# Softmax denominators of a FoX head pair: fp32 products over 128 rows, or folded to 64 rows and summed as two fp32r parts

## The chip, the cores and the metric

The kernel runs on one core of a Trainium2 chip. The metric is the device time of one execution in microseconds (us). Every line of the profile that computes is "L176", since a helper records the operations first and emits them later; tiles are therefore told apart by their names.

## The reference, cut to what matters

A two-layer decoder trunk over a sequence of 2048 tokens with model width 1024: layer 0 mixes tokens by gated linear attention (GLA), layer 1 by forgetting attention (FoX) with 16 heads of width 64. After each mixer a gated per-layer embedding (PLE) is added. The part that the change touches is the softmax of FoX:

```
logits = q . k / sqrt(d) + c[t] - c[s]          (c = cumsum(log f), causal)
probs  = softmax(logits)
o      = probs @ v
out    = (o * silu(g)) @ w_out
```

The kernel computes exp(logit - bound) without normalizing and divides the output by the sum of these exponentials over all keys: one sum for each query and head.

## The kernel before, in words

Tokens are taken in NCH = 4 chunks of T = 512 queries. Everything is held feature-major: 128 partitions by 512 tokens. fp32 precision is kept with fp32r products: an operand is split into a high part (a cast on ScalarE) and a low part (the rest, a subtraction on VectorE or GpSimd), and two or three products replace one.

**Order of the work.** The kernel is a set of generators ("streams") that `Streams.run` interleaves: `dense` (projections, output projection, PLE), `maxima` (an upper bound of each head's logits), `attention`, and short ones that are spawned with the highest priority. A stream yields what it waits for: a mark such as ("den", c, u), a free PSUM bank, or tiles that are done. The planner gives each operation a modelled start on its engine, and `flush` emits all operations in order of these starts. So every engine's order is fixed at build time, by this plan; on the chip the engines only wait for one another by semaphores. A change of one operation moves the order of all engines from there on.

**Attention.** `attention` goes through the 16 heads of a chunk. For each block of 128 keys it computes S transposed (keys on partitions, queries along the row) in a PSUM bank, exponentiates it on ScalarE into `Ph` and again in full precision, and adds the full-precision exponentials up, 128 keys by 512 queries. Two blocks in three are added by VectorE into `acc`; every third goes to GpSimd, which adds into `ag`. After the last block GpSimd adds `ag` to `acc`. So `acc` holds 128 partial sums for each query, and the sum over its 128 rows is the denominator. The products with V run two blocks later (LAG = 2) and `join` then takes the finished head.

**Denominators** (`join`, lines 1414 to 1457). Heads 2u and 2u+1 share one output tile `op`: rows 0 to 63 and 64 to 127. When the second head of a pair is done, a stream `rest` is spawned. It multiplies the two `acc` tiles in fp32 with `onesh`, two 128x128 matrices of which the first has ones in columns 0 to 63, the second in columns 64 to 127, and accumulates both into one bank `den`. Row r of this bank is then the sum of the head to which row r of `op` belongs. The bank is inverted (Ln, Exp, one Newton step), multiplied with `op` and the gate `sg`, and the result goes to the output projection, as the parts `ogh` and `ogl` or through DRAM (`os`).

**Where things wait.** `attention` waits at every odd head for the denominators of the pair before. `rest` waits for the pair's gate, ("sg1", c, u), before it takes a bank. There are three buffers of `acc` and one of `op`. `total` (line 375) is the helper that sums over partitions with two fp32r products; the q/k norms use it with `onesb` (ones in the two diagonal 64x64 blocks). Its parts `kh` and `kl` have two buffers each, which the q and k parts also use. `ple_last` keeps seven projections in buffers that attention no longer needs.

Of the kernel before, what the change touches and what calls it, by code (L numbers as in the profile page):

```python
# [11 lines left out]
F32 = mybir.dt.float32  # L12
# [8 lines left out]
P = 128  # L21
# [50 lines left out]
class Streams:  # L72
# [134 lines left out]
    def at(self, *aps):  # L207

        return self.over([self.hist[k][0] for x in aps for k in self.parts(x) if k in self.hist and self.hist[k][0]])
# [102 lines left out]
def trunk_kernel(ctx: ExitStack, tc: tile.TileContext, a: dict, out: bass.AP, layers: int = 2):  # L312
# [46 lines left out]
    def psa(name):  # L359
        return banks[sq_.take()]  # L360
# [431 lines left out]
    def ple_last(p, c):  # L792


        f, keep = L["f"], []
        for m in range(KT):
            if m % 2 == 0:
                w = wnext("wp")
            pj = yield from proj(p, w, m)
            tag = ("P0", "ag", "acc", "acc")[m // 2] if m < KT - 1 else "hx"  # L800
            keep.append((f if m < KT - 1 else acts).tile([P, T], F32, tag=tag, name="pk", bufs={"P0": 2, "ag": 2, "acc": 3, "hx": HX}[tag]))
            nc.scalar.copy(keep[m], pj)
            give(pj)
        yield ("hn1", c)

        def tail(m, pg, cs):
            e = sigmoid(pg, "ny", 2)
            give(pg)
            nc.vector.tensor_tensor(e, e, keep[m][:, cs], ALU.mult)
            nc.vector.tensor_tensor(hr[:, m, cs], hr[:, m, cs], e, ALU.add)  # L810

        s, first = SumSq(), []
        for i in range(2):
            for m in range(N_G):
                if i == 0:
                    yield bank()
                    first.append(psa("pg"))
                yield from half(first[m], og, "wg", i)
        for m in range(KT - 1):
            pg = first[m] if m < N_G else (yield from unit("pg", og, "wg"))  # L820
            tail(m, pg, slice(0, T))
            s.add(hr[:, m], nc.vector)
            if m < POOL_F:

                nc.scalar.mul(hr[:, m], hr[:, m], gcol[:, G_FIN, m : m + 1])

        w = [wnext("wg") for _ in range(2)]
        m, hw = KT - 1, T // 2
        halves = [slice(i * hw, (i + 1) * hw) for i in range(2)]
        pgs = []  # L830
        for cs in halves:
            yield bank()
            pg = psa("pg")[:, 0:hw]
            yield from steps([(w[k // 4][a][:, k % 4], og[b][:, k, cs]) for k in range(KT) for a, b in ((0, 0), (0, 1), (1, 0))], pg, 0, 24)
            tail(m, pg, cs)
            q = t2("nsq", "sq", 2)[:, 0:hw]
            nc.scalar.activation(q, hr[:, m, cs], AF.Square)
            pgs.append(q)
        for cs, q in zip(halves, pgs):
            yield bank()  # L840
            pn = psa("nq_p")[:, 0:hw]
            yield at(s.acc)
            mm(pn, ones, s.acc[:, cs], stop=False)
            yield at(q)
            mm(pn, ones, q, start=False)
            r = rsqrt(pn, 1.0 / D)
            give(pn)
            for k0 in range(0, KT, 2):
                for k in (k0, k0 + 1):
                    if k < POOL_F:  # L850
                        nc.gpsimd.tensor_tensor(hr[:, k, cs], hr[:, k, cs], r, ALU.mult)
                    else:
                        nc.vector.scalar_tensor_tensor(hr[:, k, cs], hr[:, k, cs], gcol[:, G_FIN, k : k + 1], r, ALU.mult, ALU.mult)
                nc.sync.dma_start(out[c][:, k0 : k0 + 2, cs], hr[:, k0 : k0 + 2, cs])
# [277 lines left out]
    def setup1():  # L1132
        sq_.flush()
        gx.close()
        f, fc = sbuf("f", 2), sbuf("fc", 1)
        L["f"] = f
        free.extend([fc.tile([P, 4, P], F32R, name=f"wx{x}{i}") for x in "hl"] for i in range(WX))

        L["onesb"] = fc.tile([P, P], F32R, name="onesb")
        onesb = L["onesb"].bitcast(F32)  # L1140
        nc.vector.memset(onesb, 0.0)
        nc.vector.memset(onesb[0:64, 0:64], 1.0)
        nc.vector.memset(onesb[64:128, 64:128], 1.0)
        L["onesh"] = onesh = fc.tile([P, 2, P], F32, name="onesh")
        nc.vector.memset(onesh, 0.0)
        nc.vector.memset(onesh[:, 0, 0:64], 1.0)
        nc.vector.memset(onesh[:, 1, 64:128], 1.0)

        L["lim"] = lim = fc.tile([P, T + P], BF16, name="lim")
        nc.vector.memset(lim, 0.0)  # L1150
        nc.vector.memset(lim[:, T:], -BIG)
        nc.gpsimd.affine_select(lim[:, T - P : T], lim[:, T - P : T], pattern=[[-1, P]], compare_op=ALU.is_ge, fill=-BIG, base=0, channel_multiplier=1)
        L["limT"] = limT = fc.tile([P, 2 * P], BF16, name="limT")
        nc.vector.memset(limT, 0.0)
        nc.gpsimd.affine_select(limT, limT, pattern=[[1, 2 * P]], compare_op=ALU.is_ge, fill=-BIG, base=-P, channel_multiplier=-1)
        L["qkg"] = qkg = fc.tile([P, 2], F32, name="qkg")
        nc.sync.dma_start(qkg, a["qkgain"])
        nc.vector.tensor_scalar(qkg[:, 0:1], qkg[:, 0:1], -(HD ** -0.5), None, ALU.mult)
        nc.vector.tensor_scalar(qkg[:, 1:2], qkg[:, 1:2], -1.0, None, ALU.mult)
        L["bf"] = bf = fc.tile([FH, 1], F32, name="bf")  # L1160
        nc.sync.dma_start(bf, a["fox_bf"])
        wfr = t2("wfr", "sq", 2)[:, 0 : KT * FH].rearrange("p (k n) -> p k n", n=FH)
        nc.sync.dma_start(wfr, a["fox_wf"])
        L["wf"] = wf = fc.tile([P, KT, 48], F32R, name="wf")
        nc.vector.memset(wf.bitcast(F32), 0.0)
        split(wf[:, :, 0:16], wf[:, :, 32:48], wfr, nc.vector)

        L["As"] = [fc.tile([P, T], F32R, name=f"As{i}") for i in range(NQ)]  # L1170
        L["Es"] = [fc.tile([P, T], F32R, name=f"Es{i}") for i in range(NQ)]
        L["Dm"] = [fc.tile([P, T], F32R, name=f"Dm{i}") for i in range(2)]
        L["Dc"] = [fc.tile([P, T], F32R, name=f"Dc{i}") for i in range(2)]
        for t in (*L["Es"], *L["Dm"], *L["Dc"]):
            nc.vector.memset(t[64:128].bitcast(F32), 0.0)
        for t in L["Dc"]:
            rdma(t[66:67].rearrange("o (t n) -> o t n", n=P), ones[0:4])
        for t in L["Es"]:
            nc.vector.memset(t[64:66].bitcast(F32), 1.0)
        L["carry"] = fc.tile([FH, 1], F32, name="carry")  # L1180
        nc.vector.memset(L["carry"], 0.0)

        L["KS"] = [dram.tile([FH, 130, T], F32R, name=f"KS{c}") for c in range(NCH)]

        L["QS"] = [[dram.tile([P, T], F32R, name=f"QS{h}_{c}") for c in range(NCH)] for h in range(FH)]
        L["VS"] = [[dram.tile([8, P, 4, P], F32R, name=f"VS{i}_{c}") for c in range(NCH)] for i in range(2)]
# [144 lines left out]
    def attention():  # L1331
        nxt = None
        for i in range(NCH * FH):
# [1 line left out]
            nk = 4 * (c + 1)  # L1335
            yield ("C", i)
            yield ("v", c, h // 8)
            if h % 2 and h > 1:
                yield ("den", c, h // 2 - 1)
            if nxt is None:  # L1340
                nxt = load_kv(h, 0)
            A_, E_ = L["As"][i % NQ], L["Es"][i % NQ]
            po = []
            acc = L["f"].tile([P, T], F32, tag="acc", name="acc", bufs=3)
            for kb in range(nk):
                gk, j = divmod(kb, 4)
                if j == 0:
# [66 lines left out]
    def join(c, h, po, acc):  # L1414

        i, u = h % 2, h // 2
        if i == 0:
            pair["o"] = L["f"].tile([P, T], F32, tag="op", name="op", bufs=1)
        op = pair["o"]
        own, oth = slice(i * 64, i * 64 + 64), slice(64 - i * 64, 128 - i * 64)  # L1420
        hb = t2("hb", "sq", 2)
        nc.scalar.copy(hb[own], po[oth])
        nc.vector.tensor_tensor(op[own], hb[own], po[own], ALU.add)
        give(po)
        pair[i] = acc
        if i == 0:
            return
        a0, a1 = pair[0], pair[1]

        def rest():  # L1430
            yield at(a0, a1)
            yield ("sg1", c, u)
            yield bank()
            pd = psa("den")
            mm(pd, L["onesh"][:, 0], a0, stop=False)
            mm(pd, L["onesh"][:, 1], a1, start=False)
            yq = tmp.tile([P, 2, T], F32, tag="rs", name="dn", bufs=2)
            y, q = yq[:, 0], yq[:, 1]
            nc.scalar.activation(y, pd, AF.Ln)
# [1 line left out]
            nc.vector.tensor_tensor(q, pd, y, ALU.mult)  # L1441
            give(pd)
            nc.vector.scalar_tensor_tensor(q, q, 2.0, y, ALU.subtract, ALU.mult)
            nc.vector.scalar_tensor_tensor(q, op, -1.0, q, ALU.mult, ALU.mult)
            nc.gpsimd.tensor_tensor(q, q, sgs[c, u], ALU.mult)
            if c and ("ple1", c - 1) not in sq_.marks:

                nc.sync.dma_start(os[c][:, u], q)
                later.append((c, u))
            else:  # L1450
                split(og[0][:, u], og[1][:, u], q, nc.gpsimd)
            mark(("den", c, u))
            mark(("og1", c, u))

# [156 lines left out]
```

## Time and profile before

| What | Value |
|---|---|
| Runs | 3105.07, 3113.14, 3114.41 us; median 3113.14 |
| Profiled execution | 3112.7 us, of which the span from first to last instruction is 3111.0 us |
| Granted TensorE clock, mean | 0.992 of full |
| Busy share of the span | PE 97%, weight loads 78%, DVE 72%, ACT 61%, POOL 37% |
| FoX attention runs | from about 1140 to 2971 us of the span |

PE is the matmul engine (TensorE), PEld its weight loads, DVE VectorE, ACT ScalarE, POOL GpSimd, SP the engine that issues DMAs. A matmul's record includes the time until its result is through the array, so records of a stream overlap: what a matmul takes from the engine is the distance from its start to the next one's start.

### The profile page before, as it was taken

How to read it: one execution, taken by the hardware profiler on the slowest of the kernel's cores; microseconds unless marked ns; L12 is line 12 of the kernel's file. 1: busy time of each engine (PE TensorE's matmuls, PEld its weight loads, DVE VectorE, ACT ScalarE, POOL GpSimd, SP SyncE). 2: the span in 40 equal slices, each digit the busy share in tenths (PEclk: the TensorE clock that was granted, in tenths of full speed). 3: DMA queues.
4: the chain of work that ended last, by engine and by line, in shares of the span. 5: the costliest groups of instructions: out<-in, count | busy, mean ns of one | idle time of the engine just before them, and what ended most of it. 6: DMA issues, size and time to landing. Idle time of an engine off the chain costs nothing.

```text
span 3111.0 us, 43584 instructions
## 1 busy us (share of the span) xinstructions
PE 3003.0 (97%) x13568; PEld 2412.6 (78%) x13568; DVE 2233.5 (72%) x3979; ACT 1910.6 (61%) x3651; POOL 1138.0 (37%) x941
## 2 busy tenths in 40 slices
PE   8999999999999999989999999999999999999997
PEld 6887887888788877767777777777777778788776
DVE  7686668668665765565774885884888779899845
ACT  6666666656564465654565765564776657677735
POOL 1232222213221233443333543342544435455531
PEclk9999999999999999999999999999999999999999
DMA  5565657556542658777778777767766777766674
GB/s 188 177 209 181 202 191 242 191 180 231 186 139 75 200 186 255 247 227 222 231 231 255 226 230 218 241 201 245 220 207 218 228 231 218 224 200 210 195 232 144
DMA packets 379737, 648.15 MB, mean 208 GB/s; under 512 B 43097, under 2 KB 78433, under 8 KB 379506
## 3 DMA queue, kind: packets, MB, share of 16 engines
q1 hardware_dynamic: 379506, 645.37, 65.8%
q8 instruction: 108, 1.77, 0.2%
q14 instruction: 123, 1.01, 0.1%
HBM read 521.86 MB, written 123.21 MB: 207 GB/s over the span
## 4 chain that ended last, share of the span: by engine, by line
PE 74%; DMA 11%; DVE 7%; ACT 4%; issue 2%; SPq 1%; POOL 1%; DVEq 0%; ACTq 0%; POOLq 0%
PE bank L176 74%; DMA Dm<-KS 3%; SPq L176 1%; DVE ny L176 1%; DMA wr<-gla_wv 1%; DVE rs L176 1%; DMA B<-KS 1%; DMA VS<-vv 1%; DVE wl L176 1%; ACT rs L176 1%; DMA hx<-xT 1%; DMA hx<-hs 1%; DMA KS<-kl 1%; DMA Es<-QS 1%; DMA hr<-hs 1%
## 5 line engine op out<-in xcount | busy, mean ns | idle before, releaser
L176 ACT ACTIVATE Ph<-bank 128x512 fp32r<-128x512 f32 (+2 forms) x640 | 335.1, 544 | 106.1 <-DVE bank L176 54.1
L176 DVE TENSOR_TENSOR wl<-wr,wh 128x512 fp32r<-128x512 f32 x332 | 263.7, 798 | 166.4 <-ACT wh L176 120.2
L176 PE MATMUL bank<-xnh,wh 128*128 128x512 f32 x1128 | 323.0, 394 | 0.4 <-DVE rs L176 0.4
L176 PE MATMUL bank<-xnl,wh 128*128 128x512 f32 x1128 | 323.0, 394 | 0.0
L176 PE MATMUL bank<-xnh,wl 128*128 128x512 f32 x1128 | 320.4, 393 | 0.0
L176 DVE TENSOR_REDUCE mx<-bank 128x1 f32<-128x512 f32 x384 | 249.9, 681 | 69.3 <-PE bank L176 67.6
L176 DVE TENSOR_TENSOR Pl<-bank,Ph 128x512 fp32r<-128x512 f32 (+2 forms) x400 | 245.8, 614 | 63.4 <-ACT bank L176 58.1
L176 ACT CAST wh<-wr 128x512 fp32r<-128x512 f32 x332 | 204.4, 616 | 138.7 <-PE bank L176 65.3
L176 PE MATMUL bank<-ogh,wh 128*128 128x512 f32 x912 | 258.2, 394 | 8.2 <-ACT ogh L176 7.5
L176 PE MATMUL bank<-ogh,wl 128*128 128x512 f32 x912 | 259.1, 393 | 0.0
L176 PE MATMUL bank<-ogl,wh 128*128 128x512 f32 x912 | 257.2, 392 | 0.6 <-DVE ogl L176 0.6
L176 PE MATMUL bank<-Dm,Es 128*128 128x512 f32 (+2 forms) x640 | 222.7, 376 | 35.5 <-DMA Dm<-KS 22.4
L176 PE MATMUL bank<-As,B 128*128 128x512 f32 (+2 forms) x640 | 240.6, 376 | 11.7 <-DMA B<-KS 6.6
L176 PEld LDWEIGHTS bank<-xnh,wh 128*128 128x128 f32 x1128 | 210.0, 188 | 44.9 <-DVE rs L176 1.1
L176 PEld LDWEIGHTS bank<-xnh,wl 128*128 128x128 f32 x1128 | 210.0, 188 | 43.1 <-issue 0.6
L176 PEld LDWEIGHTS bank<-xnl,wh 128*128 128x128 f32 x1128 | 209.8, 188 | 43.1 <-issue 0.7
L176 PE MATMUL bank<-Es,Dc 128*128 128x512 f32 (+2 forms) x640 | 235.0, 367 | 1.8 <-DMA Es<-mr 1.8
L176 PE MATMUL bank<-Pl,V 128*128 128x512 f32 (+2 forms) x640 | 235.7, 368 | 0.8 <-POOL Pl L176 0.5
L176 PE MATMUL bank<-Ph,V 128*128 128x512 f32 (+2 forms) x640 | 236.0, 369 | 0.0
L176 ACT ACTIVATE bank<-bank 128x512 f32<-128x512 f32 (+2 forms) x400 | 218.6, 547 | 0.0
L176 POOL TENSOR_TENSOR ag<-ag,Pf 128x512 f32<-128x512 f32 (+1 forms) x112 | 125.7, 1122 | 229.8 <-ACT Pf L176 165.0
L176 PEld LDWEIGHTS bank<-ogh,wh 128*128 128x128 f32 x912 | 171.6, 189 | 48.7 <-ACT ogh L176 10.9
(271 smaller groups left out, 7088.9 us busy)
## 6 DMA issues: line engine op xcount, KB each, us to landing
B<-KS SPq DMA_DIRECT2D x160, 256.0 KB
V<-VS SPq DMA_DIRECT2D x160, 256.0 KB
Dm<-KS SPq DMA_DIRECT2D x160, 132.0 KB
Dc<-KS SPq DMA_DIRECT2D x160, 132.0 KB
wr<-gla_wv SPq DMA_DIRECT2D x64, 256.0 KB
wr<-gla_wqk SPq DMA_DIRECT2D x64, 256.0 KB
wr<-gla_wg SPq DMA_DIRECT2D x64, 256.0 KB
wr<-gla_wo SPq DMA_DIRECT2D x64, 256.0 KB
```

Source lines behind the costliest of these rows:

```text
L176: q.emit()
```

## The change

Each finished head folds its own `acc` from 128 rows to 64: ScalarE copies the half that lies on the other head's partitions over to this head's (`fb`), GpSimd adds it to the half that is there, and the result goes to the head's half of a new tile `ds`. When both halves are there, `total` splits `ds` into two fp32r parts (ScalarE, GpSimd) and multiplies them with the block-diagonal `onesb`, which was there for the norms. `onesh` goes. `op` gets two buffers and now takes the normalized output too, in place of `q`; `acc` goes from three buffers to two. The wait for the gate moves behind the normalization. `attention` waits, at every head, for the denominators of the pair two before this one.

```diff
@@ ple_last
-            tag = ("P0", "ag", "acc", "acc")[m // 2] if m < KT - 1 else "hx"
-            keep.append((f if m < KT - 1 else acts).tile([P, T], F32, tag=tag, name="pk", bufs={"P0": 2, "ag": 2, "acc": 3, "hx": HX}[tag]))
+            tag = ("P0", "ag", "acc", "op")[m // 2] if m < KT - 1 else "hx"
+            keep.append((f if m < KT - 1 else acts).tile([P, T], F32, tag=tag, name="pk", bufs={"hx": HX}.get(tag, 2)))
@@ setup1
-        L["onesh"] = onesh = fc.tile([P, 2, P], F32, name="onesh")
-        nc.vector.memset(onesh, 0.0)
-        nc.vector.memset(onesh[:, 0, 0:64], 1.0)
-        nc.vector.memset(onesh[:, 1, 64:128], 1.0)
@@ attention
-            if h % 2 and h > 1:
-                yield ("den", c, h // 2 - 1)
+            if i > 3:
+                yield ("den", *divmod(i // 2 - 2, NP))
...
-            acc = L["f"].tile([P, T], F32, tag="acc", name="acc", bufs=3)
+            acc = L["f"].tile([P, T], F32, tag="acc", name="acc", bufs=2)
@@ join
-            pair["o"] = L["f"].tile([P, T], F32, tag="op", name="op", bufs=1)
-        op = pair["o"]
+            pair[0] = [L["f"].tile([P, T], F32, tag=x, name=x, bufs=2) for x in ("op", "ds")]
+        op, ds = pair[0]
         own, oth = slice(i * 64, i * 64 + 64), slice(64 - i * 64, 128 - i * 64)
         hb = t2("hb", "sq", 2)
         nc.scalar.copy(hb[own], po[oth])
         nc.vector.tensor_tensor(op[own], hb[own], po[own], ALU.add)
         give(po)
-        pair[i] = acc
+
+        fb = t2("fold", "sq", 2)
+        nc.scalar.copy(fb[own], acc[oth])
+        nc.gpsimd.tensor_tensor(ds[own], fb[own], acc[own], ALU.add)
         if i == 0:
             return
-        a0, a1 = pair[0], pair[1]
 
         def rest():
-            yield at(a0, a1)
-            yield ("sg1", c, u)
-            yield bank()
-            pd = psa("den")
-            mm(pd, L["onesh"][:, 0], a0, stop=False)
-            mm(pd, L["onesh"][:, 1], a1, start=False)
+            pd = yield from total("den", L["onesb"], ds, False, nc.gpsimd)
...
-            nc.vector.scalar_tensor_tensor(q, op, -1.0, q, ALU.mult, ALU.mult)
-            nc.gpsimd.tensor_tensor(q, q, sgs[c, u], ALU.mult)
+            nc.vector.scalar_tensor_tensor(op, op, -1.0, q, ALU.mult, ALU.mult)
+            yield ("sg1", c, u)
+            nc.gpsimd.tensor_tensor(op, op, sgs[c, u], ALU.mult)
             if c and ("ple1", c - 1) not in sq_.marks:
 
-                nc.sync.dma_start(os[c][:, u], q)
+                nc.sync.dma_start(os[c][:, u], op)
                 later.append((c, u))
             else:
-                split(og[0][:, u], og[1][:, u], q, nc.gpsimd)
+                split(og[0][:, u], og[1][:, u], op, nc.gpsimd)
```

The helper that the denominators now call:

```
    def total(name, w, src, square, eng):
        yield tmp.able("kh", KB)
        hl = parted(src, square, eng)
        names = {x.tensor.name for x in hl}
        tmp.held |= names
        yield at(*hl)
        yield bank()
        pn = psa(name)
        for n in range(2):
            mm(pn, w, hl[n], start=(n == 0), stop=(n == 1))
        tmp.held -= names
        return pn
```

**Two places where the order moves.** The first is PE where attention ends: the last products with V of head 15 of chunk 3, the last pair's denominators, and the output projection behind them (`ogh`, `ogl` by `wh`, `wl`; rows with `xnh` are the last gates, with `ph` a PLE projection). Before:

```order
L176 MATMUL bank_89<-Pl_8138,V_8135 128x256
L176 MATMUL bank_87<-ogh,wl_97 128x512
...
L176 MATMUL bank_94<-xnh,wh_102 128x512 x4
L176 MATMUL bank_94<-xnl,wh_102 128x512 x4
L176 MATMUL bank_94<-xnh,wl_103 128x512 x4
L176 MATMUL bank_94<-xnh,wxh_8034 128x512 x4
L176 MATMUL bank_94<-xnl,wxh_8034 128x512 x4
L176 MATMUL bank_94<-xnh,wxl_8035 128x512 x4
L176 MATMUL bank_92<-acc_8153,onesh 128x512
L176 MATMUL bank_92<-acc_8136,onesh 128x512
```

Now:

```order
L176 MATMUL bank_90<-ogh,wxh_8034 128x512 x4
L176 MATMUL bank_90<-ogl,wxh_8034 128x512 x4
L176 MATMUL bank_90<-ogh,wxl_8035 128x512 x4
L176 MATMUL bank_87<-Ph_8136,V_8134 128x256
L176 MATMUL bank_87<-Pl_8137,V_8134 128x256
L176 MATMUL bank_92<-kh_186,onesb 128x512
L176 MATMUL bank_92<-kl_187,onesb 128x512
L176 MATMUL bank_89<-ogh,wh_96 128x512 x4
L176 MATMUL bank_89<-ogl,wh_96 128x512 x4
L176 MATMUL bank_89<-ogh,wl_97 128x512 x4
```

Before, 43 other products stood between the last product with V and the denominators; now none does, and the last gates stand earlier. Behind the denominators' products come, in both, the second halves of the output projection, of which the first needs this pair's `ogh`.

The second place is ACT around a fold, in the last chunk (`sq` is the ring that `hb` and `fb` share; `Ph`, `P` and `bank<-bank` are exponentials of the next head):

```order
L176 ACTIVATE Ph_8141<-bank_91 128x512
L176 COPY sq_184<-acc_8135 64x512
L176 ACTIVATE Ph_8136<-bank_94 128x512
L176 ACTIVATE bank_94<-bank_94 128x512
L176 COPY sq_185<-bank_87 64x512
L176 ACTIVATE Ph_8139<-bank_91 128x512
L176 ACTIVATE bank_91<-bank_91 128x512
L176 ACTIVATE ag_8151<-bank_93 128x512
```

The row with `acc` is new: a copy in ACT's queue that reads what GpSimd's last addition of the head before has written, with the next head's exponentials behind it.

## Rows read from the trace of the kernel before

**Rows 1.** The page: busy time, share of the span and instructions of each engine.

```profile
PE 3003.0 (97%) x13568; PEld 2412.6 (78%) x13568; DVE 2233.5 (72%) x3979; ACT 1910.6 (61%) x3651; POOL 1138.0 (37%) x941
```

**Rows 2.** By stretch: start:end, length, PE, PEld, DVE, ACT, POOL, clock, DMA, GB/s.

```profile
1140.00:2990.00 1850.00, 1781.36 (x7887) 1415.56 (x7886) 1371.34 (x2714) 1163.10 (x2316) 831.96 (x687) 0.99 0.73 223
...
2240.00:2971.00 731.00, 714.52 (x3168) 569.26 (x3167) 626.15 (x1198) 506.31 (x1014) 376.34 (x305) 1.00 0.70 213
...
2984.00:2993.00 9.00, 6.55 (x15) 4.40 (x16) 8.32 (x9) 6.36 (x12) 5.21 (x5) 0.62 0.39 126
```

**Rows 3.** The page: chain that ended last, share by engine.

```profile
PE 74%; DMA 11%; DVE 7%; ACT 4%; issue 2%; SPq 1%; POOL 1%; DVEq 0%; ACTq 0%; POOLq 0%
```

**Rows 4.** Timeline of PE around one denominator: start, length, instruction, idle before.

```profile
1411.19 0.39 PE L176 MATMUL bank<-wh,xnl 128*128 128x512 f32 x1
...
1411.42 0.39 PE L176 MATMUL bank<-wxh,xnh 128*128 128x512 f32 x1
...
1412.93 1.88 PE L176 MATMUL bank<-acc,onesh 128*128 128x512 f32 x4
...
1413.36 0.19 PEld L176 LDWEIGHTS bank<-acc,onesh 128*128 128x128 f32 x1 [0.24 <-issue]
1413.79 0.19 PEld L176 LDWEIGHTS bank<-acc,onesh 128*128 128x128 f32 x1 [0.24 <-issue]
...
1414.88 0.39 PE L176 MATMUL bank<-wxh,xnl 128*128 128x512 f32 x1
```

**Rows 5.** Groups on PE: count | busy us, mean ns | idle before.

```profile
L176 PE MATMUL bank<-acc,onesh 128*128 128x512 f32 x128 | 60.8, 597 | 0.0
...
L176 PE MATMUL bank<-kl,onesb 128*128 128x512 f32 x64 | 26.2, 409 | 2.2 <-POOL kl L176 2.1
```

**Rows 6.** Groups on ACT from 1140 to 2990 us.

```profile
L176 ACT CAST kh<-sq 128x512 fp32r<-128x512 f32 x62 | 38.5, 621 | 2.5 <-DMA KS<-kh 0.5
...
L176 ACT COPY sq<-bank 64x512 f32<-64x512 f32 x64 | 37.2, 582 | 15.5 <-PE bank L176 14.1
...
L176 ACT ACTIVATE sq<-hr 128x512 f32<-128x512 f32 x46 | 29.0, 631 | 46.5 <-POOL hr L176 30.6 <-DVE hr L176 15.7
```

**Rows 7.** Groups on POOL and DVE from 1140 to 2990 us.

```profile
L176 POOL TENSOR_TENSOR acc<-acc,ag 128x512 f32<-128x512 f32 x64 | 84.0, 1313 | 60.3 <-DVE acc L176 26.5 <-ACT ag L176 23.4 <-PE bank L176 7.7
L176 POOL TENSOR_TENSOR kl<-sq,kh 128x512 fp32r<-128x512 f32 x62 | 82.4, 1329 | 164.4 <-ACT kh L176 150.9 <-DMA KS<-kl 6.8 <-PE bank L176 6.5
...
L176 DVE TENSOR_TENSOR op<-sq,bank 64x512 f32<-64x512 f32 x64 | 43.6, 681 | 4.7 <-ACT sq L176 3.8
```

**Rows 8.** Waits from 1140 to 2990 us: waiter, releaser, us in total, times, longest.

```profile
POOL kl L176 <- DMA KS<-kl: 34.5, 10, 8.2
...
PE bank L176 <- DMA Dm<-KS: 22.4, 21, 2.8
...
PEld bank L176 <- DVE mx L176: 14.6, 20, 1.5
...
PEld bank L176 <- ACT Ph L176: 6.7, 7, 3.7
...
PEld bank L176 <- POOL kl L176: 5.9, 11, 2.0
...
ACT Ph L176 <- POOL acc L176: 0.8, 1, 0.8
```

**Rows 9.** Tile op: ns min/median/max of the product on DVE that reads it.

```profile
L176 DVE SCALAR_TENSOR_TENSOR rs<-op,rs x32: 674/692/1765, 1223.4 to 2988.8; 128x512 f32<-128x512 f32 x32
```

**Rows 10.** Timeline of PE where attention ends.

```profile
2970.82 0.28 PE L176 MATMUL bank<-Pl,V 128*128 128x256 f32 x1
...
2980.75 1.88 PE L176 MATMUL bank<-acc,onesh 128*128 128x512 f32 x4
...
2986.94 0.80 PE L176 MATMUL bank<-ogh,wh 128*128 128x512 f32 x1 [1.09 <-ACT ogh L176]
...
2992.71 0.50 PE L176 MATMUL bank<-ogh,wh 128*128 128x512 f32 x1
```

## Prediction

> **What bounds the kernel now.** I read the page's busy times first, then its chain of waits, then busy times by stretch, the waits, and at last the timeline at single places. PE is busy for 97% of the span, the next engine, DVE, for 72% [rows 1]; in FoX attention, from 1140 to 2990 us, PE has records in 1781 of 1850 us, DVE in 1371, ACT in 1163 and POOL in 832 [rows 2]. The chain that ended last lies on PE for 74% and on DMAs for 11%; no other engine has more than 7% [rows 3]. So the kernel is bound by the number of columns that PE takes in, and what is removed there should be worth nearly its own length, unless what replaces it makes PE wait. One stretch is tighter: in the last chunk DVE is busy for 626 of 731 us and ACT for 506 [rows 2].
>
> **What goes: the fp32 products.** Two products for each of 32 pairs stand in the trace as 128 records [rows 5], two for each product, and each takes much longer than an fp32r one. Two fp32r products of 512 columns start 0.23 us apart (1411.19 and 1411.42); the weight loads between the fp32 records are 0.43 apart (1413.36 and 1413.79) [rows 4]. Over the whole place: the first of the four starts at 1412.93; the second product behind them starts at 1414.88, so the first began one step of 0.23 earlier, at 1414.65. The four take 1.72 us. In their place come two fp32r products, 0.46 us. That is 1.26 us for a pair and 32 x 1.26 = **40.3 us of PE less**. The order of the changed program bears the counts out: all 64 products with onesh are gone, and there are 32 more each of kh and kl with onesb.
>
> **What comes beside it.** On ACT each pair gets two copies of 64 rows and one cast. The cast kh<-sq takes 0.62 us and a copy of 64 rows 0.58 [rows 6], so 1.8 us a pair, 57 us in all. On POOL each pair gets two additions of 64 rows and one subtraction. No row shows 64 rows on POOL. On DVE 64 rows by 512 take 0.68 us and 128 rows have a median of 0.69 [rows 7, 9], so I take the 128-row price, 1.31 to 1.33 us [rows 7]: 3.9 us a pair, 126 us in all (half of it for the folds, 84 us in all, if POOL's price did follow the rows). The work on DVE stays the same but for three fills that go. No DMA is added; the stores of op go out in the same number as those of q did. With this POOL is busy for 958 of 1850 us and ACT for 1220, so neither becomes a bound; what counts is who waits.
>
> Three terms are set against the 40.3:
>
> *PE behind the parts.* The products used to wait for acc alone. Now they stand behind ACT's copy, POOL's fold, ACT's cast and POOL's low part. The nearest rows are the 64 sums of the q and k norms, which use the same helper: in attention PE waits 2.1 us and its loads 5.9 us for POOL's kl [rows 5, 8], 8.0/64 = 0.125 us each. The longest such wait was 2.0 us [rows 8]. So 32 of them cost 0 to 64 us; I take the mean, 4 us, since the planner puts other products in between here as there.
>
> *Busier ACT and POOL.* The largest waits of PE's loads for ACT and DVE are 6.7 us (Ph) and 14.6 us (mx) [rows 8], about 1% of what these engines are busy. 57 us more on ACT then cost 1 us, and all of them would cost 57 if ACT were a bound. DVE may also be stretched by POOL: the product that reads op takes 0.69 us in the median and up to 1.77 [rows 9], though its size is always the same. I take 4 us for all of this, for the smaller waits too.
>
> *The end of attention.* Here the order matters. Before, 43 other products stand between the last product with V and the denominators; from 2970.82 to 2992.71 PE has 57 fp32r products, 1.72 us of fp32 and a short piece to do, 15.0 us, and so loses 6.9 us, in part at a granted clock of 0.62 [rows 2, 10]. In the new order nothing is left between them, and the output projection behind needs this pair's ogh. The chain from the start of the last product is 0.28 (PE), 0.58 and 0.58 (ACT: hb and fold), 1.31 (POOL), 0.62 (ACT), 1.33 (POOL), 0.49 (PE), two ACT steps of 0.6, three DVE steps of 0.69, 1.33 (POOL) and 0.62 (ACT): 10.4 us [rows 6, 7, 9, 10]. PE has 1.1 us of work in it, so it stands for 9.3, which is 2.4 more than before. It then starts at the lower clock level, as it did before at 2986.94, where one product takes 0.80 instead of 0.39 us [rows 4, 10]; 2 us for that. I take 4.5 us; the ends are 0, if the plan on the chip fills more than the order shows, and 10.
>
> The other edits I cost at nothing. The buffers of acc (three to two) are read by POOL and ACT only, soon after a head ends, where the products once held two of them until the gate was there. The wait of attention for denominators is looser, two pairs back instead of one. With the gate behind the normalization no bank and no acc is held for it. What covers all three is that dense always has products ready; if that ran out, a head would wait one chain of some 10 us.
>
> **Sum.** 3112.7 - 40.3 + 4 + 4 + 4.5 = **3084.9, say 3085 us**. The sum is made against the profiled execution, 3112.7 us, which is 0.4 below the median of the runs, so nothing is corrected. A measurement of this kernel can tell a change of about 0.3%, 9.3 us, from none.
>
> **Rivals.**
>
> *All of it and more.* If none of the three terms shows, 3112.7 - 40.3 = 3072 us. The looser wait may also let the plan fill places where PE waits today, such as the 22.4 us for Dm [rows 8]: half of that gives 3061. For it: PE's share of the chain. Against it: those waits are for DMAs, which the change leaves alone. Chance 0.14.
>
> *POOL slows DVE.* 96 additions on POOL, each of which may stretch a DVE operation. The mechanism is in rows 9: 0.69 us in the median, 1.77 at most. If each of the 96 stretched one by a third of a microsecond, DVE would get 32 us more, and the last chunk has DVE at 86% already [rows 2]; if 20 us of that reached PE, the time would be 3084.9 + 20 = 3105. Against it: outside the last chunk DVE stands for a third of the time (745 of 1119 us busy, by the difference of the two stretches) [rows 2]. Chance 0.10. The Trainium skill (GPSIMD Engine Reference, section 1) says that GpSimd's way to SBUF is shared with VectorE, with contention for VectorE instructions that have two SBUF inputs. This speaks against the change, and the trace agrees: the product that reads op has two such inputs. By that rule at its hardest, each new addition would hold DVE for its full 1.31 us, 126 us in all; the trace's median of 0.69 says that most are not held.
>
> *The denominators' parts hold kh and kl.* There are two buffers of each for the q and k parts too, and POOL already waits 34.5 us in 10 waits for the DMAs that read kl, 3.5 each [rows 8]. If a third of the 32 pairs met such a wait and PE stood for it, 11 x 3.5 = 38 us would eat the gain: 3085 + 38 = 3123 at most, and 3113, no change, if 28 of it reached PE. Against it: denominators free their buffers by products, not DMAs. Chance 0.09.
>
> *Slower: ACT behind POOL.* The copy of acc waits in ACT's queue for POOL's last addition, and the next head's exponentials stand behind it, on which PE's products with V wait. Where ACT waits for POOL today, at sq<-hr, it loses 30.6 us over 46 operations, while for acc it lost 0.8 [rows 6, 8]. There are 64 such copies, so the gain is gone when each holds PE by 40.3/64 = 0.63 us; with one POOL step of 1.31 each, 84 us, the time would be 3112.7 - 40.3 + 84 = 3156. Against it: products run two blocks behind, and POOL is busy for less than half of the stretch. Chance 0.05.
>
> That the change does less than it says can be left out: the counts in the order show it.
>
> **How the numbers follow.** The forecast has chance 0.62, with a range of its own from 3072 to 3098. The range for 8 in 10 runs from 3066 to 3106: it takes in the forecast, the nearer half of the first rival (down to 3066), nearly all of the second, and leaves out the rest of the first, the third and the fourth, about 0.2 together. Faster by over 0.3% (below 3103.8): 0.62, 0.14 and 0.08 of the second, 0.84. Within 0.3%: 0.02 of the second and 0.08 of the third, 0.10. Slower: 0.01 of the third and 0.05 of the fourth, 0.06.
>
> **What would show it.** Right: PE's busy time falls by some 40 us or a little less (its records overlap), the waits of PE for kl grow by about 4 us, ACT waits for acc stay under 20 us in all, and there is one hole of about 9 us on PE where attention ends, with the lower clock behind it. Wrong: if ACT's copies of acc wait for POOL in most heads, if kl or ds is what PE waits for by more than 20 us, or if DVE's operations with two SBUF inputs grow well past their medians and PE's waits for DVE with them.

## The result, and the profile after

The changed kernel took 3135.9 us (median of 4 runs, 3132.4 to 3141.6) beside 3109.1 us before on the same chip (4 runs): a ratio of 1.0087, interval 1.0062 to 1.0113. It is **27 us slower** where 28 faster was forecast. The profiled execution took 3138.2 us with a span of 3136.4.

The page of the changed kernel, busy time by engine, and the chain that ended last:

```profile
PE 2989.8 (95%) x13504; PEld 2407.5 (77%) x13504; DVE 2243.3 (72%) x3976; ACT 1965.8 (63%) x3747; POOL 1265.1 (40%) x1037
...
PE 71%; DMA 11%; DVE 9%; ACT 4%; issue 2%; SPq 2%; POOL 1%; DVEq 0%; ACTq 0%; POOLq 0%
```

Against [rows 1] the additions are what was costed: ACT 55 us more (57 forecast), POOL 127 more (126). PE has 64 records and 13 us of busy time less; records overlap and get longer at a lower clock, so this is less than the 40 us of work that went. But the span less PE's busy time, which is when PE has no record at all, went from 3111.0 - 3003.0 = 108.0 to 3136.4 - 2989.8 = 146.6 us. On the chain DVE rose from 7% to 9% and PE fell by 3 points [rows 3]. So ACT's and POOL's work went as forecast, and PE idles more.

Where PE idles shows in stretches of 20 us. Four of the emptiest in attention (columns as in [rows 2]):

```profile
1520.00:1540.00 20.00, 11.25 (x26) 7.60 (x27) 19.82 (x31) 12.33 (x23) 10.42 (x9) 0.52 0.12 33
...
1820.00:1840.00 20.00, 13.03 (x39) 9.08 (x39) 16.66 (x30) 10.04 (x21) 8.52 (x7) 0.74 0.57 174
...
2020.00:2040.00 20.00, 15.09 (x54) 11.33 (x53) 16.13 (x35) 9.38 (x19) 8.61 (x7) 0.68 0.24 69
...
2800.00:2820.00 20.00, 12.95 (x41) 8.79 (x40) 18.65 (x23) 13.09 (x24) 13.83 (x9) 0.77 0.33 100
```

In the kernel before, none of the 93 such stretches from 1140 to 3000 has PE busy for less than this one:

```profile
1460.00:1480.00 20.00, 16.14 (x72) 12.76 (x70) 10.37 (x20) 3.94 (x7) 2.84 (x3) 1.00 0.82 262
```

In the first of the four DVE is busy for 19.8 of 20 us while PE has 11.3, at about half the granted clock, and the DMAs nearly rest. For these 20 us DVE is the bound. In the last DVE has 18.7; in the second and third it has 16 to 17, and no engine is at full length. Stretches with DVE at full length stood in the trace before too, with more of PE left:

```profile
2340.00:2360.00 20.00, 16.27 (x71) 12.34 (x70) 19.96 (x32) 11.43 (x23) 9.55 (x8) 1.00 0.75 242
```

Some rows of the timeline of the changed kernel around its start:

```profile
1517.31 0.40 PE L176 MATMUL bank<-Pl,V 128*128 128x512 f32 x1
...
1518.03 0.61 ACT L176 CAST kh<-ds 128x512 fp32r<-128x512 f32 x1
...
1518.33 2.41 DVE L176 SCALAR_TENSOR_TENSOR ny<-hr,gcol,rs 128x512 f32<-128x512 f32 x2
...
1518.72 1.47 POOL L176 TENSOR_TENSOR kl<-ds,kh 128x512 fp32r<-128x512 f32 x1 [1.46 <-ACT kh L176]
...
1520.66 0.68 DVE L176 TENSOR_TENSOR acc<-bank,P 128x512 f32<-128x512 f32 x1
...
1520.77 0.62 ACT L176 CAST ogh<-ny 128x512 fp32r<-128x512 f32 x1 [1.05 <-DVE ny L176]
...
1521.48 0.77 PE L176 MATMUL bank<-kh,onesb 128*128 128x512 f32 x1 [3.77 <-ACT ogh L176]
1522.05 0.63 PE L176 MATMUL bank<-kl,onesb 128*128 128x512 f32 x1
1522.47 0.63 PE L176 MATMUL bank<-As,B 128*128 128x512 f32 x1
...
1532.56 0.69 PE L176 MATMUL bank<-As,B 128*128 128x384 f32 x1 [4.08 <-DVE rs L176]
```

The end of a PLE norm (`ny`, `ogh`, `ogl`) comes in one burst on DVE, ACT and POOL, and what stands next in PE's order isn't ready in between. The product behind the hole is a new one: it belongs to a pair's denominators, whose part `kh` was cast at 1518.03 and whose `kl` was done at 1520.19. The row names ACT's `ogh`, which this product doesn't read. DVE's `acc`, which reads a bank and stands behind two `ny` in DVE's order, ended at 1521.34, just as near; the row doesn't tell which of the two it was. After the hole the products start 0.42 us apart (1522.05 and 1522.47) instead of 0.23 [rows 4]. So the hole costs twice, once as idle time and again at the lower of the two clock levels (1.2 instead of 2.4 GHz).

What PE waits for, from 1140 to 2990 us of the changed kernel:

```profile
PEld bank L176 <- DVE mx L176: 19.5, 22, 5.0
PE bank L176 <- DMA Dm<-KS: 19.5, 21, 3.2
...
PE bank L176 <- DVE acc L176: 13.6, 12, 3.0
...
PE bank L176 <- DVE mx L176: 10.2, 9, 4.5
...
PE bank L176 <- DVE Pl L176: 8.2, 5, 4.3
...
PE bank L176 <- DVE rs L176: 6.4, 3, 4.1
...
PEld bank L176 <- POOL kl L176: 4.6, 14, 0.7
...
PE bank L176 <- POOL kl L176: 0.7, 3, 0.3
```

The same view of the kernel before has for the four DVE rows:

```profile
PE bank L176 <- DVE mx L176: 3.9, 6, 1.1
...
PE bank L176 <- DVE Pl L176: 1.5, 4, 0.6
...
PE bank L176 <- DVE acc L176: 1.4, 2, 1.0
...
PE bank L176 <- DVE rs L176: 0.4, 1, 0.4
```

In these four rows PE's waits for DVE grew from 7.2 to 38.4 us, the longest from 1.1 to 4.5. Over all of PE's rows of this view its waits went from 67.5 to 97.6 us, those for DVE from 14.9 to 45.9: all of the growth. DVE has 10 us more to do in the whole kernel. What PE and its loads wait for `kl`, the norms' included, did not grow (5.3 us, 8.0 in [rows 8]). In front of the denominators' own products, sorted out by the order of the casts, PE idles for 8.3 us: 3.8 at 1521, 4.1 where attention ends, and 0.4 for the other 30 pairs together.

Where attention ends, the hole that was forecast is there. The timeline:

```profile
3018.56 0.28 PE L176 MATMUL bank<-Pl,V 128*128 128x256 f32 x1
...
3020.09 1.26 POOL L176 TENSOR_TENSOR ds<-sq,acc 64x512 f32<-64x512 f32 x1 [0.72 <-ACT sq L176]
...
3022.05 0.49 PE L176 MATMUL bank<-kh,onesb 128*128 128x512 f32 x1 [3.21 <-ACT kh L176]
...
3023.40 0.79 PE L176 MATMUL bank<-kl,onesb 128*128 128x512 f32 x1 [0.85 <-POOL kl L176]
...
3029.71 0.79 PE L176 MATMUL bank<-ogh,wh 128*128 128x512 f32 x1 [4.23 <-ACT ogh L176]
```

PE idles for 3.21 + 0.85 + 4.23 = 8.3 us. The last product with V stands at 3018.56, 48 us later than in [rows 10], and the rest behind it is 3136.4 - 3018.6 = 118 us long instead of 140: the new order leaves less output projection for the end. In front of its records PE idles for 102.0 us instead of 64.6 from the first product with V to the last, for 13.7 instead of 10.0 behind it, and for 19.6 instead of 22.2 ahead of it. So the time was lost inside attention.

### The profile page after: what moved, and what is told of

Read it like the earlier page. It is cut to its first block, busy times and chain, and to the rows that moved or that the text cites. A ratio compares the mean times of both kernels' runs of the same rounds, so it can differ in the third digit from the quotient of the medians.

```text
span 3136.4 us, 43628 instructions
## 1 busy us (share of the span) xinstructions
PE 2989.8 (95%) x13504; PEld 2407.5 (77%) x13504; DVE 2243.3 (72%) x3976; ACT 1965.8 (63%) x3747; POOL 1265.1 (40%) x1037
## 4 chain that ended last, share of the span: by engine, by line
PE 71%; DMA 11%; DVE 9%; ACT 4%; issue 2%; SPq 2%; POOL 1%; DVEq 0%; ACTq 0%; POOLq 0%
PE bank L176 71%; DMA Dm<-KS 3%; SPq L176 2%; DVE ny L176 2%; DMA B<-KS 2%; DVE rs L176 1%; DMA hx<-hs 1%; DVE mx L176 1%; DVE hr L176 1%; DVE wl L176 1%; ACT rs L176 1%; DMA VS<-vv 1%; DVE acc L176 1%; ACT Ph L176 1%; DMA wr<-gla_wv 1%
```

## Experiments

All were compared with the kernel before on the same chip. Each expectation defines its own theories. "Idle" below is the profiled span less PE's busy time: 108.0 before, 146.6 after. The order of the program hangs on the table `AFTER` (line 79), the time that the planner adds between an operation's end on an engine and its reader elsewhere:

```
before, after  {"P": 0.2,    "A": 0.15,   "V": 0.15,   "G": 0.12,   "H": 1.9}
set 4          {'P': 0.1934, 'A': 0.1583, 'V': 0.1433, 'G': 0.1229, 'H': 1.8054}
set 5          {'P': 0.2109, 'A': 0.1581, 'V': 0.142,  'G': 0.114,  'H': 1.9765}
set 9          {'P': 0.1999, 'A': 0.1564, 'V': 0.1426, 'G': 0.1182, 'H': 1.7972}
```

A set changes no operation, only the order. The sets were not drawn blindly: 4 was chosen as a good one for the changed kernel, 9 as a good one for before, and 5 was expected to be bad for before.

### The products alone, in the old order

```diff
-            mm(pd, L["onesh"][:, 0], a0, stop=False)
-            mm(pd, L["onesh"][:, 1], a1, start=False)
+            for n, x in enumerate((a0, a1)):
+                w = L["onesh"][:, n]
+                sq_.op("P", [pd], [w, x], 4 * T / 2400.0 + 0.0134, partial(nc0.tensor.matmul, pd, w, x, start=(n == 0), stop=(n == 1)))
```

`acc` and `onesh` become fp32r tiles; the planner still charges the fp32 price, so the order stays.

> The kernel before in its own order of all engines, with the two fp32 products of a pair replaced by two single fp32r ones (acc is kept in fp32r; its low parts are left out, so the denominators are rounded). No fold, no parts. Theory A (order): the 40 us of PE were real work on the path, and the loss of the changed kernel comes from its new order; here the order is kept, so 33 to 40 us faster than before (ratio 0.987 to 0.990). Theory B (the fold chain on ACT and POOL costs the time): the same here, since no fold is added. Theory C (the fp32 products only filled time in which PE would have waited): within 10 us of before.

Measured: 3112.6 us, ratio 0.9996 (0.9980 to 1.0012): nothing, as theory C had it. The page of the profiled execution, the shortest of ten (3103.4 us):

```profile
PE 2970.0 (96%) x13504; PEld 2395.3 (77%) x13504; DVE 2230.2 (72%) x3979; ACT 1909.7 (62%) x3651; POOL 1137.4 (37%) x941
```

PE's busy time fell by 33 us, and its idle time rose to 3101.6 - 2970.0 = 131.6. Waits from 1140 to 2990 us in this kernel:

```profile
PE bank L176 <- DMA Dm<-KS: 26.7, 26, 2.3
PEld bank L176 <- DVE acc L176: 19.9, 29, 2.1
...
PE bank L176 <- DMA B<-KS: 10.3, 11, 2.7
PEld bank L176 <- POOL kl L176: 8.7, 13, 1.8
```

Dm is up from 22.4, `kl` from 5.9 [rows 8]. The largest growth is in the loads' wait for DVE's `acc`; the same row before:

```profile
PEld bank L176 <- DVE acc L176: 6.5, 18, 1.4
```

Over all of PE's rows the waits rose from 67.5 to 92.7 us (DVE 14.9 to 25.4, DMAs 35.0 to 43.6). PE comes earlier to the places where DVE, POOL and DMAs hand over, and waits there.

The opposite, each fp32 product twice with ones of 0.5, in the same order:

```diff
-            mm(pd, L["onesh"][:, 0], a0, stop=False)
-            mm(pd, L["onesh"][:, 1], a1, start=False)
+                    nc0.tensor.matmul(pd, w, x, start=(n == 0), stop=False)
+                    nc0.tensor.matmul(pd, w, x, start=False, stop=(n == 1))
```

> The kernel before in its exact order on every engine, with each of the 64 fp32 products with onesh issued twice (onesh holds 0.5, so the sums are the same): 32 x 1.72 = 55 us more for PE and nothing else. With e1 this gives the slope on both sides of the same order. If PE sets the end throughout: 55 us slower, some 3168. If PE and the others are only just in balance in this order (theory A's reading of e1: the order's own waits for DVE, DMAs and POOL absorb time): 30 to 55 us slower, with PE's waits smaller than before. If other engines set the end (theory B at its strongest): under 20 us slower.

Measured: 3141.4 us, ratio 1.0089 (1.0071 to 1.0108): 28 us for 55 of PE, just under the 30 to 55 of the second reading.

```profile
PE 3052.2 (97%) x13696; PEld 2438.2 (78%) x13696; DVE 2233.4 (71%) x3979; ACT 1911.7 (61%) x3651; POOL 1139.1 (36%) x941
```

PE's idle time is 3137.9 - 3052.2 = 85.7 us, and its waits from 1140 to 2990 us are down to 46.3. In one and the same order, 55 us more on PE cost half their length, and 40 us less give nothing. PE is the busiest engine, but it doesn't set the end alone.

### The folds

```diff
-        fb = t2("fold", "sq", 2)
-        nc.scalar.copy(fb[own], acc[oth])
-        nc.gpsimd.tensor_tensor(ds[own], fb[own], acc[own], ALU.add)
+        ds = pair[1] = acc
...
-            pd = yield from total("den", L["onesb"], ds, False, nc.gpsimd)
+            pd = yield from total("den", onesr, ds, False, nc.gpsimd)
```

> The changed kernel without the folds: no copy of acc on ACT, no addition on POOL; the parts are made of the second head's acc and summed over all 128 rows, so the first head of a pair gets the second one's denominators. 64 operations on ACT and 64 on POOL go. Theory A (order): the order is still a new one with holes on PE, so it stays within 20 us of the changed kernel's 3136. Theory B (fold chain): back to 3080 to 3095, as forecast.

Measured: 3132.0 us, ratio 1.0059 (1.0036 to 1.0083). By the ratios 18 of the 27 us of loss stay without any fold, as theory A had it. But this kernel has another order again, so the folds were also taken out of the changed kernel's own order: they are planned and not issued.

```diff
-        nc.scalar.copy(fb[own], acc[oth])
-        nc.gpsimd.tensor_tensor(ds[own], fb[own], acc[own], ALU.add)
+        sq_.op("A", [fb[own]], [acc[oth]], 0.093 + T / 1200, lambda: None)
+        sq_.op("G", [ds[own]], [fb[own], acc[own]], 0.15 + T / 476, lambda: None)
```

> The changed kernel in its exact order on every engine, without the 128 fold operations (64 copies on ACT, 64 additions on POOL); the parts of the denominators are made of a constant instead, so nothing in them waits for acc, and all denominators are left out of the result (they are the same number everywhere). This cuts the chain from the last addition to acc through the fold to the denominators and takes 64 x 0.6 us from ACT and 64 x 1.3 us from POOL. Theory A (the new order as such costs the time): at most 15 us faster than the changed kernel, still over 3115. Theory B (the folds' work or the wait behind them costs it): 25 us faster or more, at or below 3110. One part must show in any case: where attention ends, PE's hole before the last denominator goes.

Measured: 3125.5 us, ratio 1.0038 (1.0022 to 1.0054). By the ratios, each to before on its own chip, 15 of the 27 us go with the folds (the two intervals allow 6 to 25) and 12 stay. That is at the edge of theory A and far from theory B. The profiled execution was the longest of six (3135.0 us):

```profile
PE 2988.2 (95%) x13504; PEld 2410.6 (77%) x13504; DVE 2233.4 (71%) x3976; ACT 1927.9 (62%) x3683; POOL 1173.5 (37%) x973
```

DVE does the same instructions in the same order and is busy for 9.9 us less than with the folds (2243.3). The four empty stretches are still there:

```profile
1520.00:1540.00 20.00, 11.59 (x41) 7.70 (x39) 19.44 (x28) 14.22 (x27) 12.01 (x9) 0.72 0.39 114
...
1820.00:1840.00 20.00, 12.94 (x38) 8.83 (x37) 16.36 (x29) 11.16 (x23) 8.82 (x8) 0.66 0.55 171
...
2020.00:2040.00 20.00, 15.16 (x57) 11.90 (x58) 14.85 (x33) 9.22 (x19) 9.06 (x7) 0.74 0.30 88
...
2800.00:2820.00 20.00, 13.01 (x42) 8.92 (x41) 18.73 (x24) 12.64 (x23) 11.92 (x9) 0.74 0.27 78
```

In the first of them the denominators' product stands behind a hole again, though its parts, made of a constant, wait for no `acc` here:

```profile
1527.11 0.47 PE L176 MATMUL bank<-kh,onesr 128*128 128x512 f32 x1 [2.25 <-DVE acc L176]
```

So the holes come without the copies and folds and without the parts' wait for `acc`. The casts and low parts are still issued, so this run doesn't tell the order from them. The part that had to show in any case came out by half: before the last denominator PE still waits 1.31 us for the cast and 0.61 for the low part, and the 4.8 us in front of the last `ogh` stay.

### The order alone

The changed kernel with set 4, and before with set 5:

> The changed kernel with the same operations in another order: only the planner's constants AFTER (what it takes a semaphore to need) are moved by up to 6%. Theory A (order): the order alone decides, so this one, in which fewer products stand behind late operands, is 25 to 45 us faster than the changed kernel, 3090 to 3110, at or a little below the kernel before. Theory B (fold chain): the folds are all there, so it stays within 10 us of 3136.

> The kernel before with the same operations in another order: only the planner's constants AFTER are moved by up to 11%. Theory A (order): 25 to 55 us slower than before (ratio 1.008 to 1.018) with no operation added, as the kernel before has an unusually good order. Theory B (fold chain): within 10 us of before.

Measured: 3085.8 us (0.9909, 0.9891 to 0.9928) and 3150.7 us (1.0125, 1.0104 to 1.0145). By the ratios the order alone moves the changed kernel by 55 us and the kernel before by 39. That is theory A in both, with more in the first than its 25 to 45 us. The page of the first:

```profile
PE 2971.1 (96%) x13504; PEld 2401.4 (78%) x13504; DVE 2229.3 (72%) x3976; ACT 1960.8 (64%) x3747; POOL 1260.8 (41%) x1037
```

Its counts are those of the changed kernel, and PE's idle time is 3084.1 - 2971.1 = 113.0 us instead of 146.6. The slow one of before has empty stretches like those of the changed kernel as given, with DVE at full length:

```profile
2960.00:2980.00 20.00, 14.08 (x48) 8.52 (x46) 19.83 (x22) 16.73 (x33) 15.83 (x11) 0.92 0.82 256
2980.00:3000.00 20.00, 10.46 (x33) 6.93 (x33) 19.44 (x38) 6.21 (x14) 7.33 (x7) 0.67 0.36 125
```

The missing halves of these pairs, and a third set for both kernels:

> The kernel before with the constants AFTER of e4, so the same rule for the order as in e4 on the operations of before: the pair e4 minus this one is the change at another setting of the order. Theory A (the change as such is worth little, and every set of constants deals a new order worth some 20 us up or down): anywhere from 3090 to 3135; over the four pairs (the two kernels given, and three more sets) the change's mean effect lies within 12 us of nothing, with both signs among them. Theory B (the changed kernel's operations cost time in any order): below 3075, that is e4 is slower by over 10 us, as in each of the pairs. Theory C (the operations save what was forecast, and only the order of the changed kernel as given was bad): e4 is faster by 20 to 40 us, 3106 to 3126 here, and as much in the other new pairs.

> The changed kernel with the constants AFTER of e5 (before's operations took 3150.7 us with them). Theory A: anywhere from 3105 to 3150. Theory B: above 3160. Theory C: 3110 to 3130.

> The kernel before with a third set of constants AFTER, {'P': 0.1999, 'A': 0.1564, 'V': 0.1426, 'G': 0.1182, 'H': 1.7972}, chosen from as many sets for before as those that e4's set was chosen from for the changed kernel. All theories: faster than before, 3085 to 3110, since the same choosing gained e4 50 us over the changed kernel as given. Theory A: not more than 20 us behind e4's 3085.8. Theory C: 20 to 40 us behind e4, since the best order of the cheaper operations should be that much better.

> The changed kernel with the third set of constants, the one chosen for before in e9. Theory A: within 30 us of e9, more likely slower, since the set was chosen for before. Theory B: slower than e9 by over 10 us, as in all pairs. Theory C: faster than e9 by 10 us or more.

Measured, with those from above (ratio to before, interval; idle time of PE in us):

| Order | before's operations | changed kernel | difference |
|---|---|---|---|
| as given | 1; 108.0 | 1.0087 (1.0062 to 1.0113); 146.6 | +0.9% |
| set 4 | 1.0008 (0.9993 to 1.0023); 100.9 | 0.9909 (0.9891 to 0.9928); 113.0 | -1.0% |
| set 5 | 1.0125 (1.0104 to 1.0145); 132.2 | 0.9999 (0.9985 to 1.0013); 128.9 | -1.3% |
| set 9 | 0.9938 (0.9919 to 0.9956); 85.4 | 1.0026 (1.0011 to 1.0041); 137.0 | +0.9% |
| mean | 1.0018; 106.6 | 1.0005; 131.4 | -0.1% |

By the ratios the change is a gain of 31 and 39 us in two orders and a loss of 27 in two. Theory A holds (both signs, a mean of 4 us); theory B (a loss in each) fails with sets 4 and 5, theory C (a gain in each new pair) with set 9. The idle times are of one profiled execution each; that of before with set 9 was the shortest of its runs (3078.6 us, median 3090.0), so 85.4 is on the low side. Over the four PE idles for 25 us more with the changed kernel, and its busy time is 25 us less (3004.8 to 2979.5); the mean spans, 3111.5 and 3110.9, are the same. The mean of four such differences has a standard error of some 0.6%, 18 us, and the sets were chosen, not drawn. The forecast, 0.9% faster, lies 1.3 standard errors from this mean: on the mean, nothing, the forecast and a small loss are all still possible. The best of each side, 3085.8 and 3090.0 us, both beat the two kernels given.

### What 40 us of PE are worth in a new order

The cheap products of the first experiment again, with the planner told what they cost:

```diff
-                sq_.op("P", [pd], [w, x], 4 * T / 2400.0 + 0.0134, partial(nc0.tensor.matmul, pd, w, x, start=(n == 0), stop=(n == 1)))
+                sq_.op("P", [pd], [w, x], T / 2400.0 + 0.0134, partial(nc0.tensor.matmul, pd, w, x, start=(n == 0), stop=(n == 1)))
```

> The kernel before with each denominator made by two single fp32r products of acc (acc itself is kept in fp32r; its low parts are left out), as in e1, but now the planner is told their true price, so that every engine gets a new order around the 40 us that PE no longer needs. No folds, no parts, the old wait of attention. Theory A (the order decides: work taken from PE is worth something only when the other engines' work is ordered anew around it): 20 to 35 us faster than before, some 3078 to 3094, with PE's idle time after 1100 us not above that of before. Theory B (PE is only just the bound; DVE, ACT, POOL and the DMAs come next at the same length, so nothing is gained in whatever order): within 10 us of before, with PE's waits for DVE and POOL grown by the 40 us, as in e1.

Measured: 3095.9 us, ratio 0.9943 (0.9922 to 0.9964): 17 us, between the theories. The other three sets:

> e6 (cheap products of acc without folds or parts, their true price known to the planner; the low parts of acc are left out) with e4's constants. With e6 and the two other sets it gives the mean over four orders, against the mean of before over the same four. Theory A1 (40 us less on PE are worth something on the mean, and the folds and parts give it back): the mean over the four is 15 to 35 us below that of before; single orders differ by up to 30. Theory A2 (PE is so near balance with the others that 40 us less are worth nothing in any order): the means lie within 10 us.

> The same with e5's constants, where the operations of before took 3150.7 us. A1: with the others a mean 15 to 35 us below that of before; A2: within 10 us.

> The same with e9's constants, where the operations of before took 3090 us. A1: with the others a mean 15 to 35 us below that of before; A2: within 10 us. At this set, which was chosen for before, the pair itself may well be slower.

Measured: 1.0074 (1.0046 to 1.0102) with set 4, 0.9923 (0.9901 to 0.9945) with set 5, 1.0036 (1.0020 to 1.0052) with set 9. The mean of the four is 0.9994, against 1.0018 of before: 7 us of gain, within the 10 us of A2, with a standard error of some 0.7%, so that A1's 15 to 35 us are not excluded. Idle time is 131.2 us on the mean, as with the changed kernel. So these four give no support to the chance that, on the mean, the folds and parts eat a gain that the cheap products alone would bring. The kernel without folds at set 4:

> e3 (the changed kernel without folds: the parts are made of the second head's acc of a pair alone, so the first head's denominator is not its own) with e4's constants. If the folds give the gain back: over the four sets the mean of this is as far below before as that of the cheap products, 15 to 35 us. If the parts do (cast on ACT, low part on POOL, two products that wait for them): the mean is within 10 us of before's and of the changed kernel's.

Measured: 3127.4 us, 1.0047 (1.0025 to 1.0069); one order, which says no more than that its swing is of the same size. The other two sets were not tried with it.

## Why the prediction was wrong

**The step that failed is the price of PE's time**: "what is removed there should be worth nearly its own length". The 40.3 us were right as work and wrong as time. In the old order on every engine, with PE's work less and nothing else, the gain is 0.04% (at most 0.2% by the interval), not 1.3%. "97% busy" was read as "sets the end"; yet PE runs in step with DVE, POOL and the DMAs, and where it comes early it waits for them: its waits in attention are 92.7 us with less work on PE in one order, 67.5 as given and 46.3 with more. The rows that spoke for it were on the table: a chain with 26% off PE, and DVE at 86% in the last chunk [rows 2, 3].

Beside this gain that did not come stands the loss of 27 us: 15 go with the folds, and for the other 12 no run separates the new order, the parts, and the new waits and buffers. These 12 us are less than what another order alone does to either kernel. In the changed kernel's waits DVE waits for nothing before it writes `acc`, so the buffer less of `acc` holds DVE nowhere.

**The missing term is the order.** The text before the prediction says that one changed operation moves all engines' orders, and the sum had no term for it. "What covers all three is that dense always has products ready" was an assumption on the new order, and at 1517 and 1528 us nothing that stood next in PE's order was ready. Its size is shown by sets that move only the order: from -0.6% to +1.3% for before's operations and from -0.9% to +0.9% for the changed kernel's. A range of 40 us with no such term could hold the time only by luck. Why this order has the bursts and that one hasn't was not taken further than the timeline.

**Terms that were right or small.** *PE behind the parts*: 4 us forecast as a mean of 0.125 each; PE idles for 4.2 in front of these products before the end of attention, 3.8 of it in one place, so the sum came out by luck. *The end of attention*: PE idles for 8.3 us where 9.3 were forecast, and the lower clock follows (0.79 us for the product at 3029.71). Behind the last product with V it idles for 3.7 us more than before, beside the 2.4 that were forecast. *Busier ACT and POOL*: the work came as counted. The sum's 4 us for its effect was too small: without the folds, in the same order, the kernel is 15 us faster.

**The rivals.** *The parts hold kh and kl*: POOL waits 26.6 us for the DMAs that read `kl`, less than the 34.5 of [rows 8]. *POOL slows DVE*: DVE's busy time grew by 9.8 us beside 127 us more of POOL, and the product that reads `op` kept its median, as did `ny` (747 ns, 746 before):

```profile
L176 DVE SCALAR_TENSOR_TENSOR op<-op,rs x32: 674/691/1693, 1223.2 to 3027.0; 128x512 f32<-128x512 f32 x32
...
L176 DVE SCALAR_TENSOR_TENSOR ny<-hr,gcol,rs x24: 735/747/1787, 1518.3 to 2814.9; 128x512 f32<-128x512 f32 x24
```

Against [rows 9] the median didn't move. Yet single operations take up to 1.8 us. One is among the two `ny` ahead of the hole at 1521, which took 2.41 us together while POOL made `kl`. And in the changed kernel's own order DVE's busy time is 9.9 us less without POOL's folds. So the rival's mechanism is there, at a third of its 32 us; how much of it reached PE no run tells. Of the signs of being wrong, half of one came: PE's waits for DVE grew, by 31.0 us, and DVE's medians didn't. The Trainium skill (GPSIMD Engine Reference, section 1) has GpSimd and VectorE share their way to SBUF; by that rule at its hardest DVE would have got 126 us, and this trace has 10. *Slower: ACT behind POOL* had the sign and not the place: ACT's `Ph` waits for POOL's `acc` in no row of the changed kernel, and POOL's fold waits for ACT instead (53.5 us in 44 waits). That the sign of the fourth rival came true is no merit of its mechanism.

## What to carry to other kernels

An engine that is 97% busy in a program with a fixed order isn't thereby the bound: scan short stretches for another engine at full length beside it, and price what is removed by a run in the same order before planning around it. Where any edit makes a planner redraw the order, take the spread over a few redrawn orders as the noise of every comparison (here about 1% either way), and judge an edit by several orders, or choose the order first. Here the choice of the order moved the time of either kernel by nearly 2% from best to worst, more than the change did in any one order.

## What was not expected of the hardware

POOL's addition on 64 rows takes as long as on 128 (groups on POOL from 1140 to 3030 us of the changed kernel):

```profile
L176 POOL TENSOR_TENSOR ds<-sq,acc 64x512 f32<-64x512 f32 x64 | 83.8, 1309 | 54.4 <-ACT sq L176 53.5
L176 POOL TENSOR_TENSOR acc<-acc,ag 128x512 f32<-128x512 f32 x64 | 83.4, 1303 | 28.2 <-DVE acc L176 18.8 <-PE bank L176 7.8 <-ACT ag L176 1.1
```

A fold to half the rows saves POOL nothing here; the prediction had taken this price without a row that showed it. And PE's clock makes holes dearer: the mean granted clock went from 0.992 to 0.985, and 0.007 of 3136 us is 22 us at full speed. By estimate that is an upper bound (PE also idles in these stretches) for what the lower level adds to the holes before it. No run here separates the two.
